# Hybrid mLSTM/HGRN2 step on one core: later transposes and mixing in the mains, more early output blocks, and v's gate weights behind the projected block

## The chip, the cores and the metric

The kernel runs on one core of one Trainium2 chip. Such a core has five engines that each work through their own instructions in order: TensorE (PE: matmuls and transposes, with its weight loads as PEld), VectorE (DVE), ScalarE (ACT), GpSimd (POOL) and SyncE (SP), which here only issues DMAs. Tiles lie in SBUF (128 partitions), matmuls write to PSUM banks, and inputs, outputs and scratch tensors lie in HBM. The metric is the device time of one launch in microseconds (us); lower is better.

## What is computed

One decoder layer on a prompt of 1024 tokens and on 8 samples of 8 tokens, 1088 rows of width 1024 in all. After an RMSNorm, one projection gives seven groups of 1024 columns; four mLSTM heads and eight HGRN2 heads run as causal recurrences, evaluated in chunks; both are normalised, gated, joined and projected back.

```python
xn = rmsnorm(x, g_norm)
xm, zm, om, fh, qh, ih, zh = split(xn @ w_in)
xc = silu(causal_conv(xm, conv_buf, conv_w, conv_b))
q, k, v = per_head(xc @ w_q), per_head(xc @ w_k), per_head(xm @ w_v)
gates = concat(q, k, v) @ w_gate + b_gate
hm, C1, n1, m1 = mlstm_scan(q, k, v, gates[:4], log_sigmoid(gates[4:]), C0, n0, m0)
hm = (layernorm(hm) * sigmoid(om) + m_skip * xc) * silu(zm)
logf = log(lb + (1 - lb) * sigmoid(fh))
oh, S1 = hgrn2_scan(silu(qh), (1 - lb) * sigmoid(-fh), ih, logf, S0)
oh = rmsnorm(oh) * silu(zh)
y = rmsnorm(x + concat(hm, oh) @ w_out, g_final)
```

The outputs are y for prompt and samples, and the new convolution rows, C, n, m and S of both.

## The kernel before

**Arithmetic.** float32 products are made of splits: each operand is a rounded high part plus a rest, and `mm3` (L94 to L96) sums three matmuls, high x high, rest x high, high x rest. ScalarE rounds (the high part); GpSimd or VectorE subtracts (the rest).

**Front.** The normalised rows lie transposed and split in XH and XL. A block is 128 columns of `w_in`: `in_block` runs 24 matmuls in each of three stretches of tokens (384, 384, 320) and hands the bank to an evacuation. For each mLSTM head the two xm blocks are projected and convolved (`front_conv`); v is made from xm (`front_v`), q and k from the convolved xc (`front_qk`), and all three go to HBM. `qkv_prep(h)` loads and splits the head's weights, and folds the gate weights into eight further columns of v's weights: four transposes of w_v (L394), a copy (wT, L395), two matmuls (L398), a copy (gv, L401), two transposes back (L403), and two VectorE passes into the split weights (L405, L406). `front_v` (L488) then finds the gates' part of v in columns 256 to 264 of its bank; VectorE copies or adds it into GTOK (L505, L507) while ScalarE copies v (L503).

**Mains.** Twelve mains follow, in the order H0 M0 H1 M1 H2 M2 H3 M3 H4 H5 H6 H7. `mlstm_main` runs eight chunk steps with the state C (split into CC, L749 and L750), a `layer_norm` of each step's result into a tile hn (L657), its transposes (`turn_back`, L719) and the product onto om (L724); then the samples' stage (transposes L811, state updates L821 to L825), and at its end, for two feature tiles, the mixing: load xcr, multiply-add with om (VectorE, L837), multiply with zm (GpSimd, L839), store to mixd. `hgrn_main` starts with Q and K (L972, L973, L937), a first run of small matmuls (L101, called by `burst`), then `products(n)` for n = 2 to 64 (VectorE: L1005, L940, L1008, L1010), the matmuls of the lower levels (2, 4, 8), of the upper levels (16, 32, 64), and then state, outputs and norms. `gate_scan` runs its scans on VectorE beside the first main.

**Order.** In the mains TensorE's order is written by hand: `weave` takes a main, which yields after each piece the matmul time that should follow it, and emits that much (times a ratio) of the side work, which is the next job's projection blocks, 48 pieces a main. The ratio is the side's cost over the main's sum of yields (`HEAD`, 47.2 for H and 53.4 for M, plus an extra where other work is woven in), so that both end together. The other engines' order comes from a scheduler that simulates the program ahead of time and goes by the order in which instructions were emitted, as far as buffers and operands allow; it is fixed in the program, and `issue_after` adds an edge to it on one engine. Outside the mains TensorE's order comes from it too.

**Buffers.** Large tiles come from one pool of 18 units; PSUM has three pools, mm (3 banks, projections and output accumulators), lv (2) and o (3). Weight and mix loads share three buffers (wraw).

**Output.** The output projection sums 15 mixed tiles from HBM and the last head's z from SBUF, in two column halves (hf) and nine row blocks (t). Five blocks of the first half are begun beside the last main (`early_out`): their accumulators are closed and stored as partial sums for t = 0 and 1 (`out_store`), and stay open in the three mm banks for t = 2 to 4. After the last main, `out_done(0, t)` adds the last tile, the residual and the sum of squares (L1318, L1322), and the blocks t = 5 to 8 follow one by one from t = 2 on, each with a load of the second half's weights (`wo_prep`). `wo_split` (L1241) subtracts on GpSimd for odd tiles of the first half, else on VectorE.

Of the kernel before, what the change touches and what calls it, by code (L numbers as in the profile page):

```python
# [9 lines left out]
F32 = mybir.dt.float32  # L10
# [20 lines left out]
def hybrid_step(  # L31
# [345 lines left out]
    def qkv_prep(h):  # L377

        wr = qkv_load(h)
        wh = unit("wqh", F32R)  # L380
        wl = unit("wql", F32R)
        whv, wlv = vcols(wh), vcols(wl)
        wrv = wr[:, 512:1024].rearrange("p (a c) -> p a c", c=256)
        S.copy(wh[:, :512], wr[:, :512])
        S.copy(whv[:, :, :256], wrv)
        G.tensor_tensor(wl[:, :512], wr[:, :512], f32(wh[:, :512]), op=ALU.subtract)
        G.tensor_tensor(wlv[:, :, :256], wrv, f32(whv[:, :, :256]), op=ALU.subtract)
        qkv_w[h] = (wh, wl)
        wT = half("wT")
        pt = ps_o()  # L390
        for b in range(2):
            for a in range(2):
                o, i = 512 + a * 256 + b * P, b * 2 + a
                PE.transpose(pt[:, i * P:(i + 1) * P], wr[:, o:o + P], ident)  # L394
        V.tensor_copy(wT[:, :512], pt)  # L395
        pg = ps_o()
        for b in range(2):
            PE.matmul(pg[:8, :256], lhsT=wgr[:, 8 + 2 * h + b, :], rhs=wT[:, b * 256:(b + 1) * 256],  # L398
                      start=b == 0, stop=b == 1)
        gv = sp.tile([P, 256], F32, tag="hn", name=nm("gv"), bufs=3)  # L400
        V.tensor_copy(gv[:8, :], pg[:8, :256])  # L401
        for a in range(2):
            PE.transpose(pg[:, 256 + a * 8:264 + a * 8], gv[:8, a * P:(a + 1) * P], ident[:8, :8])  # L403
        pgv = pg[:, 256:272].rearrange("p (a c) -> p a c", c=8)
        V.tensor_copy(whv[:, :, 256:264], pgv)  # L405
        V.tensor_tensor(wlv[:, :, 256:264], pgv, f32(whv[:, :, 256:264]), op=ALU.subtract)  # L406

    GTOK = cp.tile([P, 9, 8], F32, name="GTOK")

# [78 lines left out]
    def front_v(h):  # L488
        wh, wl = qkv_w[h]
        xms = [fr[2 * h + a]["m"] for a in range(2)]  # L490
        for t in range(9):
# [12 lines left out]
            if h:  # L504
                V.tensor_tensor(GTOK[:, t, :], GTOK[:, t, :], ps[:, 256:264], op=ALU.add)  # L505
            else:
                V.tensor_copy(GTOK[:, t, :], ps[:, 256:264])  # L507
            if t == 8:
                nc.sync.dma_start(out=vsd[h], in_=vt[:, :VW])
            elif u:  # L510
                nc.sync.dma_start(out=vd[h, :, (t - 1) * VW:(t + 1) * VW], in_=vt[:, :2 * VW])

# [28 lines left out]
    def gate_scan():  # L541
# [21 lines left out]
        yield 4.0  # L563
# [14 lines left out]
        yield 4.0  # L578
# [80 lines left out]

    def mlstm_main(h):  # L660
# [70 lines left out]
        C = tp = hn = None  # L731
        for j in range(8):
# [18 lines left out]
            if j > 0:  # L751
                if j % 2:
                    tp = ps_lv()
                turn_back(hn, tp, (j - 1) % 2)
                if j % 2 == 0:
                    onto_om(tp, j // 2 - 1)
            hn = layer_norm(pn, j, h)
# [3 lines left out]
            yield 2.8 if j else 4.2  # L761
        turn_back(hn, tp, 1)
        onto_om(tp, 3)
# [32 lines left out]
        yield 5.0  # L796
        pn = ps_o()
# [10 lines left out]
        yield 3.0  # L808
        tp = ps_lv()
        for a in range(2):  # L810
            PE.transpose(tp[:, a * P:(a + 1) * P], hn[:, a * P:(a + 1) * P], ident)  # L811
        for a in range(2):
            oms, ts = compact(d["om"][a][:, TP:T]), spread(tp[:, a * P:(a + 1) * P])
            for e in range(2):
                V.scalar_tensor_tensor(oms[:, e], ts[:, e], mln[:, 2 * h + a:2 * h + a + 1], oms[:, e],
                                       op0=ALU.mult, op1=ALU.mult)
        for a in range(4):
# [9 lines left out]
            yield 1.3  # L827
# [4 lines left out]
        for a in range(2):  # L832
# [3 lines left out]
            with tc.issue_after(getattr(new, "ins", new)):  # L836
                V.scalar_tensor_tensor(xc[:, :T], xc[:, :T], msk[:, ft:ft + 1], d["om"][a][:, :T],  # L837
                                       op0=ALU.mult, op1=ALU.add)
            G.tensor_tensor(xc[:, :T], xc[:, :T], d["zm"][a][:, :T], op=ALU.mult)  # L839
            nc.sync.dma_start(out=mixd[ft], in_=xc[:, :T])  # L840
            yield 1.8
# [75 lines left out]
    def hgrn_main(h):  # L917
# [78 lines left out]
        small_out(ps, 288, 1, 1)  # L996
        yield 1.0
# [61 lines left out]
        for n in (2, 4, 8):  # L1059
            lower.append(products(n))  # L1060
            yield 3.3
# [172 lines left out]
    def wo_split(hf, i):  # L1234
# [6 lines left out]
        (G if hf == 0 and i % 2 else V).tensor_tensor(lo, raw, f32(hi), op=ALU.subtract)  # L1241
# [38 lines left out]
    def out_part(hf, t, g):  # L1280
# [6 lines left out]
        for k in range(len(mx)):  # L1287
            stop = (hf, t, g, k) in ((0, 0, 1, 6), (0, 1, 1, 6))
# [10 lines left out]
    def out_store(t):  # L1299

        if t == 0:
            part[1] = unit("xr")
        part[t] = part[1][:, t * HU:(t + 1) * HU]
# [48 lines left out]
    HEAD = {"H": 47.2, "M": 53.4}  # L1352
# [20 lines left out]
    EARLY = 5  # L1373

    def early_out():
        for t in range(EARLY):
# [5 lines left out]
            if t < EARLY - 3:  # L1382
                out_store(t)

    side = chain(*[(hgrn_in if kind == "H" else mlstm_in)(h) for kind, h in jobs], early_out())
    qkv_prep(0)
    run(front_conv(0, (0, 1)))
    for h in range(4):
        front_v(h)
        if h < 3:  # L1390
            qkv_prep(h + 1)
        if h < 3:
            run(front_conv(h + 1, (2 * h + 2,)))
        else:
# [9 lines left out]
    with tc.manual_schedule(engines={mybir.EngineType.PE}):  # L1404
        for i, (kind, h) in enumerate(jobs[:-1]):
            main = (hgrn_main if kind == "H" else mlstm_main)(h)
            extra = 0.0
            if i == 0:
                main, extra = with_gates(main, gates), 9.0
            weave(islice(side, STEPS), main, us / (HEAD[kind] + extra))  # L1410
        weave(side, hgrn_main(7), (us / 2 + EARLY * cost(45, 512)) / HEAD["H"])
        for t in range(9):
            out_done(0, t)
            if EARLY - 3 <= t < 6:
                run(chain(out_part(0, t + 3, 0), out_part(0, t + 3, 1)))
# [97 lines left out]
```

## Time and profile before

| | |
|---|---|
| median of 3 runs | 1219.85 us (1218.01 to 1223.15) |
| the profiled execution's own time | 1220.89 us |
| its span in the trace | 1219.1 us |
| instructions | 22869 |
| mean granted TensorE clock | 0.983 |
| bytes read from and written to HBM | 93.96 and 38.43 MB |

The span runs from the first to the last instruction in the trace. A row of TensorE's waits names the waiting tile and line, then the engine, tile and line that released it, and gives the total, the number and the longest wait. Windows give busy time by engine in a stretch and the clock that TensorE was granted in it (1.00 is full speed). A row of the timeline gives start and length in us, engine, line, the tiles, and in brackets the idle time just before it with what ended it; rows with "xN" are several instructions merged.

### The profile page before, as it was taken

The numbers are of one execution on the slowest core, as the hardware profiler recorded it, in microseconds if no ns is written. First come the engines' busy times: TensorE is split into PE (matmuls) and PEld (weight loads), VectorE is DVE, ScalarE is ACT, GpSimd is POOL, SyncE is SP. The second block draws the span as 40 slices with busy tenths as digits, with TensorE's granted clock in tenths as the row PEclk, the third lists the DMA queues.
The fourth block names the chain that finished last, engine by engine and source line by source line (L and its number), as shares of the span: only waits on it lengthen the run. The fifth ranks groups of instructions, "written<-read, shape, count | busy, mean of one in ns | idle before, by whom it ended". The sixth has DMA issues, their size and how long they took to land. (4 is left out here: it accounts for less than half of the span.)

```text
span 1219.1 us, 22869 instructions
## 1 busy us (share of the span) xinstructions
PE 1139.4 (93%) x9251; PEld 1064.6 (87%) x9251; DVE 771.5 (63%) x1474; ACT 437.4 (36%) x937; POOL 389.3 (32%) x508
## 2 busy tenths in 40 slices
PE   6899999979988999899998999899999989989997
PEld 5789999979988998899988998899999978767886
DVE  4674544595669466875669466876868686533443
ACT  5454444425321443134321453142424233333332
POOL 4443333223434343523434352533232331100000
PEclk9899999999999999999999999999999999989999
DMA  8133334123133232414132331412121245556652
GB/s 262 45 129 134 129 122 135 35 54 125 60 115 107 84 114 74 148 53 146 34 120 98 110 106 57 143 54 73 53 74 53 73 143 141 166 157 180 210 175 99
DMA packets 154061, 133.89 MB, mean 110 GB/s; under 512 B 11439, under 2 KB 130155, under 8 KB 153954
## 3 DMA queue, kind: packets, MB, share of 16 engines
q1 hardware_dynamic: 153954, 132.41, 34.6%
q8 instruction: 73, 1.20, 0.4%
q14 instruction: 34, 0.28, 0.1%
HBM read 93.96 MB, written 38.43 MB: 109 GB/s over the span
## 5 line engine op out<-in xcount | busy, mean ns | idle before, releaser
L94 PE MATMUL mm<-XH,whi 128*128 128x384 f32 (+1 forms) x1344 | 454.3, 338 | 0.9 <-DVE z L880 0.6
L95 PE MATMUL mm<-XL,whi 128*128 128x384 f32 (+1 forms) x1344 | 442.6, 329 | 0.0
L96 PE MATMUL mm<-XH,wlo 128*128 128x384 f32 (+1 forms) x1344 | 442.1, 329 | 0.0
L94 PEld LDWEIGHTS mm<-XH,whi 128*128 128x128 f32 x1344 | 255.7, 190 | 5.7 <-issue 1.7
L95 PEld LDWEIGHTS mm<-XL,whi 128*128 128x128 f32 x1344 | 255.9, 190 | 1.7 <-issue 1.3
L96 PEld LDWEIGHTS mm<-XH,wlo 128*128 128x128 f32 x1344 | 255.0, 190 | 0.0
L147 POOL TENSOR_TENSOR wlo<-wraw,whi 128x1024 fp32r<-128x1024 f32 x56 | 139.5, 2491 | 226.5 <-ACT whi L147 226.0
L147 ACT CAST whi<-wraw 128x1024 fp32r<-128x1024 f32 x56 | 58.9, 1051 | 123.4 <-PE mm L95 104.5
L94 PE MATMUL mm<-XH,mhi 128*128 128x512 f32 x144 | 59.2, 411 | 10.1 <-ACT lv L1322 4.6
L96 PE MATMUL mm<-XH,mlo 128*128 128x512 f32 x144 | 57.8, 401 | 1.2 <-DVE mlo L1267 1.2
L1266 ACT CAST mhi<-mraw 128x1024 fp32r<-128x1024 f32 (+1 forms) x32 | 31.9, 998 | 74.7 <-PE mm L95 56.2
L95 PE MATMUL mm<-XL,mhi 128*128 128x512 f32 x144 | 57.7, 401 | 0.0
L1335 POOL TENSOR_TENSOR rs<-rs,mhalf 128x1 f32<-128x1 f32 (+1 forms) x9 | 4.9, 542 | 158.3 <-DVE rs L1334 158.3
L1267 DVE TENSOR_TENSOR mlo<-mraw,mhi 128x1024 fp32r<-128x1024 f32 (+1 forms) x32 | 39.0, 1221 | 24.0 <-ACT mhi L1266 23.8
L940 DVE TENSOR_TENSOR QK<-hk,Sf 128x256 f32<-128x256 f32 x96 | 49.4, 555 | 0.0
L457 DVE TENSOR_TENSOR xml<-mm,xmh 128x384 fp32r<-128x384 f32 (+1 forms) x24 | 12.1, 508 | 52.2 <-ACT XB L456 45.0
L872 DVE TENSOR_SCALAR f<-f,OML,LB 128x384 f32<-128x384 f32 (+1 forms) x24 | 26.8, 1116 | 27.2 <-ACT f L870 27.1
L94 PEld LDWEIGHTS mm<-XH,mhi 128*128 128x128 f32 x144 | 27.9, 194 | 17.2 <-issue 5.0
L1008 DVE TENSOR_TENSOR Sf<-Sf,f 128x512 f32<-128x512 f32 (+1 forms) x48 | 40.1, 836 | 0.1
L892 ACT COPY iT<-mm 128x128 f32<-128x128 f32 x64 | 13.0, 270 | 73.3 <-PE mm L96 70.3
L473 DVE SCALAR_TENSOR_TENSOR Y<-XB,PAR,Y 128x1112 f32<-128x1112 f32 x24 | 38.1, 1589 | 0.2
L96 PE MATMUL mm<-woh,mlo 128*128 128x512 f32 x96 | 37.5, 391 | 0.3 <-DVE mlo L1267 0.3
(350 smaller groups left out, 2237.0 us busy)
## 6 DMA issues: line engine op xcount, KB each, us to landing
wraw<-in_w_in SPq DMA_DIRECT2D x56, 512.0 KB, 4.2
woraw<-in_w_out SPq DMA_DIRECT2D x16, 512.0 KB, 4.4
mraw<-mixd SPq DMA_DIRECT2D x16, 512.0 KB, 6.2
mraw<-mixd SPq DMA_DIRECT2D x16, 448.0 KB, 4.5
xcd<-XB SPq DMA_DIRECT2D x8, 544.0 KB, 2.7
qkd<-qk SPq DMA_DIRECT2D x16, 272.0 KB, 5.0
xcr<-xcd SPq DMA_DIRECT2D x8, 544.0 KB
mixd<-xcr SPq DMA_DIRECT2D x8, 544.0 KB
```

Source lines behind the costliest of these rows:

```text
L94: PE.matmul(out, lhsT=lh, rhs=rh, start=first, stop=False)
L95: PE.matmul(out, lhsT=lh, rhs=rl, start=False, stop=False)
L96: PE.matmul(out, lhsT=ll, rhs=rh, start=False, stop=last)
L147: return S.copy(hi, raw), G.tensor_tensor(lo, raw, f32(hi), op=ALU.subtract)
L457: V.tensor_tensor(ml[:, t0:t0 + m], ps[:, :m], f32(mh[:, t0:t0 + m]), op=ALU.subtract)
L473: V.scalar_tensor_tensor(Y[:, :1112], XB[:, j:j + 1112], cw[:, 8 * j + ft:8 * j + ft + 1], Y[:, :1112], op0=ALU.mult, op1=ALU.add)
L872: V.tensor_scalar(f[:, s], f[:, s], scalar1=OML[:, h:h + 1], scalar2=LB[:, h:h + 1], op0=ALU.mult, op1=ALU.add)
L892: S.copy(dst, ps[:, u * P:(u + 1) * P])
L940: i = V.tensor_tensor(dst, ksrc, ssrc, op=ALU.mult)
L1008: V.tensor_tensor(hv(Sf, W, n)[:, :, 0, :], hv(Sf, W, n)[:, :, 0, :], hv(f, W, n)[:, :, 1, n - 1:n].to_broadcast([P, ng, n]), op=ALU.mult)
L1266: S.copy(hi[:, :w * n], raw[:, :w * n])
L1267: V.tensor_tensor(lo[:, :w * n], raw[:, :w * n], f32(hi[:, :w * n]), op=ALU.subtract)
```

## The change

It touches six places.

- `qkv_prep` becomes a generator of two parts: loads and splits first, v's gate columns second. The caller emits the second part behind the block that is projected meanwhile (for head 0 behind both xm blocks).
- `front_v`: ScalarE copies the gate columns, into GTOK for head 0, else into a new tile GST, which VectorE adds to GTOK once at the end.
- `mlstm_main`: each hn is transposed two steps later instead of one, the last one behind the samples' preparation; the samples' transposes go between their state updates; the yields change, and the mixing leaves the main as two deferred pieces.
- `hgrn_main` takes up these pieces behind products(2) and products(4) when it follows an mLSTM main, with 1.8 of yield each (an extra of 3.6).
- `gate_scan` yields 5.5 twice instead of 4.0 (the first main's extra: 12 instead of 9).
- Output: VectorE subtracts in every `wo_split`; four early blocks are stored instead of two, two in a unit; the later blocks begin behind `out_done(0, 3)`.

```diff
     def qkv_prep(h):
...
         qkv_w[h] = (wh, wl)
+        yield
         wT = half("wT")
...
         V.tensor_tensor(wlv[:, :, 256:264], pgv, f32(whv[:, :, 256:264]), op=ALU.subtract)
+        yield
     def front_v(h):
...
             S.copy(vv[:, u, 0:256], ps[:, :256])
-            if h:
-                V.tensor_tensor(GTOK[:, t, :], GTOK[:, t, :], ps[:, 256:264], op=ALU.add)
-            else:
-                V.tensor_copy(GTOK[:, t, :], ps[:, 256:264])
+            S.copy((GST if h else GTOK)[:, t, :], ps[:, 256:264])
...
+        if h:
+            V.tensor_tensor(GTOK, GTOK, GST, op=ALU.add)
     def gate_scan():
-        yield 4.0
+        yield 5.5
...
-        yield 4.0
+        yield 5.5
     def mlstm_main(h):
-        C = tp = hn = None
+        C = tp = None
+        hns = []
         for j in range(8):
...
-            if j > 0:
+            if j > 1:
+                if j % 2 == 0:
+                    tp = ps_lv()
+                turn_back(hns.pop(0), tp, j % 2)
                 if j % 2:
-                    tp = ps_lv()
-                turn_back(hn, tp, (j - 1) % 2)
-                if j % 2 == 0:
                     onto_om(tp, j // 2 - 1)
-            hn = layer_norm(pn, j, h)
+            hns.append(layer_norm(pn, j, h))
...
-            yield 2.8 if j else 4.2
-        turn_back(hn, tp, 1)
-        onto_om(tp, 3)
+            yield 2.8
+        tp = ps_lv()
+        turn_back(hns.pop(0), tp, 0)
...
         yield 5.0
+        turn_back(hns.pop(0), tp, 1)
+        onto_om(tp, 3)
...
         hn = layer_norm(pn, 8, h)
-        yield 3.0
-        tp = ps_lv()
-        for a in range(2):
-            PE.transpose(tp[:, a * P:(a + 1) * P], hn[:, a * P:(a + 1) * P], ident)
...
+        yield 2.0
         for a in range(4):
...
-            yield 1.3
+            if a == 1:
+                tp = ps_lv()
+                for b in range(2):
+                    PE.transpose(tp[:, b * P:(b + 1) * P], hn[:, b * P:(b + 1) * P], ident)
+                for b in range(2):
+                    oms, ts = compact(d["om"][b][:, TP:T]), spread(tp[:, b * P:(b + 1) * P])
+                    for e in range(2):
+                        V.scalar_tensor_tensor(oms[:, e], ts[:, e], mln[:, 2 * h + b:2 * h + b + 1], oms[:, e],
+                                               op0=ALU.mult, op1=ALU.mult)
+            yield 1.5
...
-        for a in range(2):
+        def mixed(a):
             ft = 2 * h + a
             xc = unit("xcr")
             nc.sync.dma_start(out=xc[:, :T], in_=xcd[ft])
-            with tc.issue_after(getattr(new, "ins", new)):
-                V.scalar_tensor_tensor(xc[:, :T], xc[:, :T], msk[:, ft:ft + 1], d["om"][a][:, :T],
-                                       op0=ALU.mult, op1=ALU.add)
+            V.scalar_tensor_tensor(xc[:, :T], xc[:, :T], msk[:, ft:ft + 1], d["om"][a][:, :T],
+                                   op0=ALU.mult, op1=ALU.add)
             G.tensor_tensor(xc[:, :T], xc[:, :T], d["zm"][a][:, :T], op=ALU.mult)
             nc.sync.dma_start(out=mixd[ft], in_=xc[:, :T])
-            yield 1.8
+        deferred.extend([lambda: mixed(0), lambda: mixed(1)])
     def hgrn_main(h):
+        late = [deferred.pop(0) for _ in range(len(deferred))]
         yield 1.0
...
         for n in (2, 4, 8):
             lower.append(products(n))
+            if late:
+                with tc.issue_after(getattr(lower[-1][3], "ins", lower[-1][3])):
+                    late.pop(0)()
+                yield 1.8
             yield 3.3
     def wo_split(hf, i):
-        (G if hf == 0 and i % 2 else V).tensor_tensor(lo, raw, f32(hi), op=ALU.subtract)
+        V.tensor_tensor(lo, raw, f32(hi), op=ALU.subtract)
     def out_part(hf, t, g):
-            stop = (hf, t, g, k) in ((0, 0, 1, 6), (0, 1, 1, 6))
+            stop = hf == 0 and t < STORED and (g, k) == (1, 6)
     def out_store(t):
-        if t == 0:
-            part[1] = unit("xr")
-        part[t] = part[1][:, t * HU:(t + 1) * HU]
+        if t % 2 == 0:
+            ctxs["xr"] = unit("xr")
+        part[t] = ctxs["xr"][:, t % 2 * HU:(t % 2 + 1) * HU]
-    HEAD = {"H": 47.2, "M": 53.4}
+    HEAD = {"H": 47.2, "M": 48.2}
-    EARLY = 5
+    EARLY, STORED = 5, 4
     def early_out():
-            if t < EARLY - 3:
+            if t < STORED:
                 out_store(t)
-    qkv_prep(0)
+    prep = qkv_prep(0)
+    next(prep)
     run(front_conv(0, (0, 1)))
+    run(prep)
     for h in range(4):
         front_v(h)
         if h < 3:
-            qkv_prep(h + 1)
+            prep = qkv_prep(h + 1)
+            next(prep)
             run(front_conv(h + 1, (2 * h + 2,)))
+            run(prep)
...
             extra = 0.0
+            if kind == "H" and i and jobs[i - 1][0] == "M":
+                extra = 3.6
             if i == 0:
-                main, extra = with_gates(main, gates), 9.0
+                main, extra = with_gates(main, gates), 12.0
             weave(islice(side, STEPS), main, us / (HEAD[kind] + extra))
...
             out_done(0, t)
-            if EARLY - 3 <= t < 6:
-                run(chain(out_part(0, t + 3, 0), out_part(0, t + 3, 1)))
+            if 3 <= t < 7:
+                run(chain(out_part(0, t + 2, 0), out_part(0, t + 2, 1)))
```

More of the change, by code (lines that the diff above doesn't have):

```diff
@@ L406, in qkv_prep @@
         V.tensor_tensor(wlv[:, :, 256:264], pgv, f32(whv[:, :, 256:264]), op=ALU.subtract)
+        yield
     GTOK = cp.tile([P, 9, 8], F32, name="GTOK")
+    GST = cp.tile([P, 9, 8], F32, name="GST")
     def gate_part(h, qk, ready):
@@ L658, in layer_norm @@
         return hn
+    deferred = []
     def mlstm_main(h):
@@ L807, in mlstm_main @@
         hn = layer_norm(pn, 8, h)
-        yield 3.0
-        tp = ps_lv()
-        for a in range(2):
-            PE.transpose(tp[:, a * P:(a + 1) * P], hn[:, a * P:(a + 1) * P], ident)
-        for a in range(2):
[L813 to L816, printed above, removed]
+        yield 2.0
         for a in range(4):
@@ L831, in mlstm_main @@
             G.tensor_copy(NEWv[:, h, 4 * i:4 * i + 4], C0v[i][:, :, 256])
-        for a in range(2):
+        def mixed(a):
             ft = 2 * h + a
@@ L1390, in hybrid_step @@
         if h < 3:
-            qkv_prep(h + 1)
-        if h < 3:
+            prep = qkv_prep(h + 1)
+            next(prep)
             run(front_conv(h + 1, (2 * h + 2,)))
+            run(prep)
         else:
```

## The prediction

> **What bounds the kernel now.** I read the first part of the page, then TensorE's own view of waits, then windows around each wait for the granted clock.
>
> ```profile
> span 1219.1 us, 22869 instructions
> PE 1139.4 (93%) x9251; PEld 1064.6 (87%) x9251; DVE 771.5 (63%) x1474; ACT 437.4 (36%) x937; POOL 389.3 (32%) x508
> ```
>
> TensorE is busy for 1139.4 of 1219.1 us. The change takes no matmul away, so all it can win lies in the 79.7 us in which TensorE stands, and in slow clock around these gaps. TensorE's waits (us in total, times, longest):
>
> ```profile
> PE lv L719 <- DVE hn L657: 15.3, 16, 1.6
> PE lv L101 <- DVE K L937: 13.3, 4, 3.3
> ...
> PE mm L94 <- ACT lv L1322: 4.6, 1, 4.6
> PE lv L101 <- DVE QK L1005: 4.6, 2, 2.8
> PE mm L94 <- DVE z L880: 4.3, 3, 3.7
> PE o L398 <- DVE wT L395: 2.9, 2, 2.1
> PE mm L94 <- DVE GTOK L507: 2.7, 2, 2.2
> PE lv L811 <- DVE hn L657: 2.7, 4, 0.7
> ...
> PE mm L94 <- DVE xr L1318: 1.7, 2, 0.9
> ...
> PE mm L94 <- DVE GTOK L505: 1.3, 4, 0.6
> PE mm L1276 <- DVE xr L1318: 1.1, 1, 1.1
> ```
>
> Each of these lines belongs to one part of the change. The windows (length, busy time of PE, PEld, DVE, ACT, POOL, then PEclk, DMA share, GB/s) show what follows a gap:
>
> ```profile
> 36.00:46.00 10.00, 7.54 (x43) 5.44 (x42) 6.62 (x20) 5.14 (x13) 3.37 (x17) 0.70 0.18 52
> 60.00:68.00 8.00, 5.85 (x33) 5.08 (x32) 5.24 (x10) 3.94 (x9) 3.83 (x3) 0.79 0.40 132
> 264.00:274.00 10.00, 5.95 (x116) 5.21 (x114) 8.43 (x14) 3.02 (x10) 3.68 (x8) 0.83 0.40 107
> 786.00:792.00 6.00, 5.95 (x98) 5.82 (x99) 5.93 (x14) 0.00 (x0) 1.28 (x3) 0.72 0.31 90
> 990.00:1000.00 10.00, 6.32 (x24) 5.04 (x23) 9.90 (x19) 2.10 (x2) 0.08 (x1) 0.83 0.39 121
> 1066.00:1074.00 8.00, 4.65 (x11) 3.71 (x12) 3.20 (x6) 2.41 (x8) 0.00 (x0) 0.59 0.86 269
> ```
>
> A clock of 0.72 over 6 us is 0.28 x 6 = 1.7 us of work not done; in the same way 3.0, 1.7, 1.7, 1.7 and 3.3 us in the others, of which some falls on idle time.
>
> **The mLSTM mains (four of them).** Before, the transposes of step j's normalised tile (L719) are emitted in step j+1; now in j+2, and the sample's (L811) two matmul pairs later. What a step gets between is its yield times the weave's ratio: 2.8 x 47.4/53.4 = 2.5 us before, 2.8 x 47.4/48.2 = 2.75 us now (47.4 us is what the kernel's own cost formula gives for four blocks, 4 x 24 matmuls over 1088 columns). The longest wait on hn is 1.6 us, so one whole step more covers it: 15.3 + 2.7 = 18.0 us go. What is late next is the split state CC, which step j+1 multiplies:
>
> ```profile
> 719.26 0.73 DVE L750 TENSOR_TENSOR CC<-C,CC 128x258 fp32r<-128x258 f32 x1
> ...
> 721.44 0.28 PE L94 MATMUL o<-CC,qgl 128*128 128x258 f32 x1
> ```
>
> It is there 1.45 us ahead in step 1, where the step shrinks from 4.2 x 47.4/53.4 = 3.7 us to 2.75: 1.0 us less, just enough. These waits also gave VectorE time to catch up, so I let 1 us per main come back: bounds 0 and 3 us; 14 us net.
>
> **From an mLSTM main to the next HGRN2 main.** L101 waits 3.3 us four times. VectorE's order there, and then the same entry where no mLSTM main stands before it:
>
> ```profile
> 774.51 1.35 DVE L837 SCALAR_TENSOR_TENSOR xcr<-xcr,PAR,om 128x1088 f32<-128x1088 f32 x1
> ...
> 776.24 3.40 DVE L837 SCALAR_TENSOR_TENSOR xcr<-xcr,PAR,om 128x1088 f32<-128x1088 f32 x1
> ...
> 777.13 0.31 PE L96 MATMUL mm<-XH,wlo 128*128 128x320 f32 x1
> ...
> 779.56 0.47 DVE L880 TENSOR_TENSOR hq<-hq,mm 128x320 f32<-128x320 f32 x1
> 780.07 2.76 DVE L973 TENSOR_TENSOR Q<-hq,f 128x544 f32<-128x544 f32 x1
> 782.75 3.11 DVE L937 COPY K<-hk 128x256 f32<-128x256 f32 x2
> ...
> 786.01 0.65 PE L101 MATMUL lv<-Q,K 128*32 128x64 f32 x32 [3.34 <-DVE K L937]
> ```
>
> ```profile
> 845.74 2.18 DVE L973 TENSOR_TENSOR Q<-hq,f 128x544 f32<-128x544 f32 x1
> ...
> 847.85 1.19 DVE L937 COPY K<-hk 128x256 f32<-128x256 f32 x2
> ```
>
> The two L837 (1.35 + 3.40) stand ahead of the last hq, of Q and of K. The change takes them out. hq's block ends on TensorE at 777.4, and with half a microsecond for ScalarE's half (an estimate: VectorE's is 0.47) hq could start at 777.95, 1.6 us earlier than it did. K's copies shrink from 3.11 towards 1.19, Q from 2.76 towards 2.18: 2.5 us more, 4.1 in all against a wait of 3.34. TensorE comes 5.0 x (1.004 - 0.933) = 0.35 us sooner, as the entry's yield has a lower ratio (47.4/50.8). I take a rest of 0.3 us: 3.0 us each, and the 1.7 us of slow clock behind it: 4.7 x 4 = 19 us.
>
> The Trainium skill (TensorE: Matmul & The Clock Gate, "Why this matters for your kernels") would have the clock drop only after idle gaps over some 3 us. The trace differs: the window at 264 us holds a longest gap of 2.8 us and a clock of 0.83. By the rule a rest of up to 3 us would still win the clock back; by the trace a rest of 2.8 us would not, and the sum would be 4 x 1.7 = 7 us smaller. A rest of 0.3 wins it by both.
>
> **Where the two L837 go.** They, their two GpSimd multiplies, and on SP's queue their loads and stores now stand in the HGRN2 main, after products(2) and products(4), with 1.8 of yield each. Such a pass costs more than itself, as this pair shows:
>
> ```profile
> 984.88 5.19 POOL L1241 TENSOR_TENSOR XL<-woraw,XH 128x1024 fp32r<-128x1024 f32 x2 [7.50 <-DMA woraw<-in_w_out]
> ...
> 985.18 5.19 DVE L940 TENSOR_TENSOR QK<-hk,Sf 128x256 f32<-128x256 f32 x2
> ...
> 993.38 1.22 DVE L1241 TENSOR_TENSOR XL<-woraw,XH 128x1024 fp32r<-128x1024 f32 x1
> ```
>
> VectorE's work stands until GpSimd's pass is through (5.19 beside 5.19). So a deferred pair costs VectorE between 2 x 1.35 = 2.7 and about 2 x (1.35 + 5.19/2) = 7.9 us. Its cover:
>
> ```profile
> 794.22 0.68 DVE L1005 TENSOR_TENSOR QK<-hq,f 128x512 f32<-128x512 f32 x1
> ...
> 801.95 1.16 PE L101 MATMUL lv<-QK 128*32 128x32 f32 x112
> ```
>
> The lower levels' last operand is ready at 794.9, TensorE asks at 801.95: 7.05 us, less 1.7 (the slow clock that is gone) and 0.9 (12.9 of yield at the lower ratio), plus 3.6 x 0.933 = 3.4: 7.8 us. That is just the dearest case, so 0 to 2 us per main; I take 0.5, 2 us in all. Mains and entries together: 14 + 19 - 2 = **31 us** (15 to 37).
>
> **The front.** The waits on wT (2.9) and GTOK (2.7 + 1.3) and the clock of the first two windows (3.0 + 1.7) make 11.6 us.
>
> ```profile
> 41.62 1.88 PE L398 MATMUL o<-wT,front 128*8 128x256 f32 x4 [2.12 <-DVE wT L395]
> ...
> 62.64 0.22 ACT L459 COPY XB<-mm 128x64 f32<-128x64 f32 x1 [3.43 <-DVE xml L457]
> ```
>
> Behind the projected block, the chain transpose, wT, L398, gv, L403, copies has the next block and front_qk to hide in for h = 1 to 3. For h = 0 nothing is left but front_v, which needs it, and the convolution's passes now stand ahead on VectorE: 0 to 6 us come back there. ScalarE gets 36 copies of 8 columns; the nearest row is 0.22 us for 64 columns, so at most 36 x 0.22 = 8 us on an engine that is busy for 36% of the span, in place of 36 VectorE steps on which TensorE waited. Net between -3 and 10; I take **4 us**.
>
> **The gate scan in the first main.** 3 more units of yield, mostly ahead of L1005's two waits (4.6), against a ratio that falls from 0.84 to 0.80: **1 us** (-1 to 4).
>
> **The last HGRN2 main.** The odd GpSimd passes L1241 become VectorE passes of 1.22. The pair above held VectorE for 5.19; two passes of 1.22 and L940's own work (some 0.7, an estimate from the 0.68 of L1005 over as many columns) replace this, 2.0 us less ahead of the z of L880 on which TensorE stood 3.7 us, and part of the 1.7 us of clock: **3.5 us** (0 to 7).
>
> **The output's start.** Four blocks are stored early, not two, so accumulators are free when t = 5 begins.
>
> ```profile
> 1066.33 0.68 DVE L1318 TENSOR_TENSOR xr<-xr,o 128x512 f32<-128x512 f32 x1
> ...
> 1069.35 0.76 PE L94 MATMUL mm<-XH,mhi 128*128 128x512 f32 x1 [4.64 <-ACT lv L1322]
> ```
>
> The 4.6 us, the 1.7 and the 1.1 on xr, and about 2 us of slow clock after 1069 can go, 9.4 us. The fourth out_done still needs the first's bank in a pool of three, which L1318 frees, and one more weight load goes ahead of t = 5's mix load on SP; the two further residual loads go early, beside the last main. **6 us** (1 to 9).
>
> **Sum.** 31 + 4 + 1 + 3.5 + 6 = 45.5 us off the profiled execution, whose time is 1220.9 (its span and 1.8 us around it): 1175.4. The median of the runs is 1219.85, 1 us under it, so 1174 to 1175; I say 1175.
>
> **The rivals.**
> - *VectorE is late in the HGRN2 mains.* The Trainium skill (SBUF — State Buffer, Terms) has VectorE and GpSimd lock each other out for a whole instruction; the 5.19 beside 5.19 agrees. If all four GpSimd passes of a main (two deferred, two weight splits) fall on the products, 2 us of wait and 1.7 of clock return per main: 15 us, 1190. For: cover and price are equal to 0.1 us. Against: the dear case needs every pass to collide. Chance 0.15.
> - *The mains don't pack.* The hn waits reappear on CC and the entries keep their clock loss: 14 us, the 7 of clock and half of the entries' 13 come back: 27, 1203. Against: all but one step gets longer. Chance 0.08.
> - *The front's chain lies open* for h = 0, with slow clock after it: 7 us back, 1182. Chance 0.07.
> - *Slower: the deferred load is stuck on SP.*
>
> ```profile
> 785.06 14.55 SPq L140 DMA_DIRECT2D wraw<-in_w_in  x2
> ```
>
> SP issues in order and here stands 14.55 us before a weight load can go. If the second xcr load is issued behind it, VectorE stands at L837 with the products queued behind, and TensorE at the lower levels. From 12 us of net wait per main all is lost; with 14.55 less what is left of the cover after the passes (0 to 2), it is 13 x 4 + 7 of clock after longer gaps = 59 us: 1234. Against: the row waits for a weight buffer; a load whose own buffer is free earlier is issued ahead of it. Chance 0.06. A milder form gives back about all: 1216, 0.04.
>
> **How the numbers follow.** The forecast has 0.60; its own range is 1165 to 1186. Faster by over 0.5% (about what a measurement can tell from no change): 0.60 + 0.15 + 0.08 + 0.07 = 0.90; within: 0.04; slower: 0.06. The range 1162 to 1203 leaves out the last two rivals and the best corner, some 0.15.
>
> **What would show it.** Right: hn L657 and K L937 gone from TensorE's waits, the entry windows at clock 1.00, L837 between the products, no wait of L101 at the lower levels, no GTOK or wT, no L1322 near the output's start. Wrong: new rows of L101 behind QK or xcr, of L94 behind CC, a gap before front_v(0), or xcr as VectorE's releaser by a DMA.

## The result, and the profile after

| | before | after |
|---|---|---|
| median | 1220.7 us (1218.0 to 1223.2, 4 runs) | 1190.6 us (1188.6 to 1191.6, 4 runs) |
| after / before | | 0.975, 95% interval 0.973 to 0.978 |
| span of the profiled execution | 1219.1 us | 1188.1 us |

The kernel became 30 us faster. The forecast was 1175 us with a range of 1162 to 1203, so the time lies in the range, and 15.6 us above the forecast: almost on the 1190 us of the first rival.

The head of the page after:

```profile
span 1188.1 us, 22927 instructions
PE 1130.5 (95%) x9251; PEld 1062.1 (89%) x9251; DVE 782.3 (66%) x1447; ACT 441.1 (37%) x973; POOL 381.9 (32%) x504
```

VectorE is busy for 10.8 us longer than before (771.5), with 27 instructions fewer. That is the first hint. TensorE's waits after (released by; us in total, times, longest):

```profile
...
PE lv L1123 <- ACT A L1066: 10.5, 5, 3.2
PE lv L101 <- DVE QK L950: 7.9, 4, 2.2
PE mm L94 <- DVE z L890: 6.2, 1, 6.2
...
PE mm L95 <- DVE wql L407: 2.2, 1, 2.2
PE o L399 <- DVE wT L396: 2.1, 1, 2.1
PE mm L94 <- DVE wqh L406: 1.4, 1, 1.4
PE lv L101 <- DVE K L947: 1.1, 1, 1.1
```

Most rows that the change aimed at are gone: no hn (18.0 us before), K only once, no GTOK, no wait at the output's start (L1322 and xr before). The wait for head 0's wT is still there, 2.1 us as before. In place of the others stand two rows that come five and four times, in the HGRN2 mains: the upper levels' end (L1123) behind A, and the lower levels (L101) behind QK. wqh and wql are new in the front, and there is one wait of 6.2 us for z, in the first main, where there were three with 4.3 in all.

Where the gain arose can be read from marks in TensorE's timeline: the first small matmul of a HGRN2 main (`lv<-Q,K`), the first matmul of an mLSTM main (`lv<-q,k`), and the first of `out_done` (`o<-XH,zh`). All numbers are us of the profiled executions.

| stage, from mark to mark | before | after | change | predicted |
|---|---|---|---|---|
| front, to H0 | 231.08 | 230.15 | -0.9 | -4 |
| H0 with the gate scan, to M0 (302.81; 303.17) | 71.73 | 73.02 | +1.3 | -1 |
| M0 to H5 (849.18; 833.13) | 546.37 | 529.96 | -16.4 | -31 |
| H5 to H7 (974.80; 958.78) | 125.62 | 125.65 | 0.0 | 0 |
| H7 to `out_done` (1062.51; 1040.90) | 87.71 | 82.12 | -5.6 | -3.5 |
| `out_done` to the end | 156.59 | 147.20 | -9.4 | -6 |
| sum | 1219.1 | 1188.1 | -31.0 | -45.5 |

The whole gap lies in one row: M0 to H5, 14.6 us short. The front and the first main missed by 5.4 us, the last two stages made that good by 5.5. Within M0 to H5 an mLSTM main with its side work went from 75.6 us (M1: 514.13 - 438.58) to 65.4 (499.60 - 434.17), while the HGRN2 main ahead of it went from 60.5 (438.58 - 378.11) to 65.4 (434.17 - 368.73). Between its marks the HGRN2 main runs six of the projection's matmuls more (282 for 276), which is about 1 us; the other 4 us are loss.

The timeline of after in H3, a main that took up the two mixing pieces (start, length, engine, line, tiles; in brackets the idle time ahead and its releaser):

```profile
628.67 2.17 DVE L983 TENSOR_TENSOR Q<-hq,f 128x544 f32<-128x544 f32 x1
630.76 1.20 DVE L947 COPY K<-hk 128x256 f32<-128x256 f32 x2
...
635.52 1.35 DVE L846 SCALAR_TENSOR_TENSOR xcr<-xcr,PAR,om 128x1088 f32<-128x1088 f32 x1 [0.66 <-DMA xcr<-xcd]
...
636.95 2.54 POOL L848 TENSOR_TENSOR xcr<-xcr,zm 128x1088 f32<-128x1088 f32 x1 [3.83 <-DVE xcr L846]
...
637.16 2.92 DVE L1019 TENSOR_TENSOR Sf<-Sf,f 128x544 f32<-128x544 f32 x1
...
642.39 0.71 DVE L1019 TENSOR_TENSOR Sf<-Sf,f 128x544 f32<-128x544 f32 x1
...
643.78 1.34 DVE L846 SCALAR_TENSOR_TENSOR xcr<-xcr,PAR,om 128x1088 f32<-128x1088 f32 x1
...
645.20 2.92 POOL L848 TENSOR_TENSOR xcr<-xcr,zm 128x1088 f32<-128x1088 f32 x1 [5.71 <-DVE xcr L846]
...
645.64 5.26 DVE L950 TENSOR_TENSOR QK<-hk,Sf 128x256 f32<-128x256 f32 x2
...
648.09 2.53 POOL L147 TENSOR_TENSOR wlo<-wraw,whi 128x1024 fp32r<-128x1024 f32 x1
...
650.96 0.46 PE L101 MATMUL lv<-QK 128*32 128x32 f32 x32 [1.79 <-DVE QK L950]
...
652.61 0.75 DVE L950 TENSOR_TENSOR QK<-hk,Sf 128x256 f32<-128x256 f32 x2
```

The entry is as forecast: Q 2.17 and K 1.20, no wait. Then come the pieces. Beside the first multiply L848, L1019 takes 2.92 us where its twin takes 0.71. Beside the second one and the weight split right behind it (2.92 + 2.53), the two L950 take 5.26 where they take 0.75 seven us later. What TensorE waits for at 650.96 is exactly this L950. So in this main VectorE lost 1.35 + 1.34 to the pieces themselves, 0.66 to the load, 2.2 and 4.5 to being held: 10.1 us, of which some 2.5 belong to the weight split. The prediction had 7.9 as the dearest price against 7.8 of cover.

The second half of the same main:

```profile
660.86 2.40 POOL L147 TENSOR_TENSOR wlo<-wraw,whi 128x1024 fp32r<-128x1024 f32 x1
...
661.03 2.77 DVE L1021 TENSOR_TENSOR f<-f 128x512 f32<-128x512 f32 x1
...
666.45 0.28 DVE L1103 TENSOR_TENSOR Vs<-V,Vs 128x128 fp32r<-128x128 f32 x1
...
666.77 1.28 ACT L1107 ACTIVATE VL<-Vs,CF 128x128 fp32r<-128x128 f32 x4 [4.11 <-DVE Vs L1103]
667.96 1.80 ACT L1066 COPY A<-lv 32x128 f32<-32x128 f32 x6
...
669.81 0.66 PE L1123 MATMUL lv<-CF,iT 128*128 128x128 f32 x4 [2.70 <-ACT A L1066]
```

VectorE is still late, and a second weight split holds it again (L1021 takes 2.77 us where it took 0.69 nine us earlier), so Vs comes late; ScalarE stands 4.11 us for it with VL at the head of its queue, and the copies of A (L1066) are queued behind VL. TensorE's row names ScalarE, but ScalarE was itself held by VectorE.

Windows of after (length; PE, PEld, DVE, ACT, POOL busy; clock; DMA share; GB/s):

```profile
763.00:769.00 6.00, 6.00 (x111) 5.97 (x112) 5.41 (x9) 0.60 (x3) 1.42 (x3) 1.00 0.71 256
...
669.00:677.00 8.00, 7.19 (x52) 7.19 (x53) 3.31 (x10) 4.08 (x9) 1.14 (x2) 1.00 0.03 6
802.00:810.00 8.00, 8.00 (x41) 8.00 (x42) 3.01 (x9) 2.38 (x7) 0.00 (x0) 0.63 0.00 0
...
303.20:833.10 529.90, 511.74 (x4484) 498.31 (x4482) 393.08 (x811) 180.23 (x417) 219.37 (x267) 0.99 0.30 97
```

The entry of H4 has the full clock (0.72 before), but the clock now falls behind the new wait in the same main, 0.63 over 8 us, 3.0 us of work not done; in H3, at 669 us, it held. The last row is the stretch M0 to H5, and here it is for the kernel before:

```profile
302.80:849.20 546.40, 515.06 (x4493) 499.61 (x4493) 378.59 (x811) 178.68 (x416) 215.18 (x267) 0.99 0.29 95
```

TensorE stands for 546.4 - 515.1 = 31.3 us before and 18.2 after. VectorE executes 811 instructions in both, but is busy 14.5 us longer.

### The profile page after: what moved, and what is told of

Same layout as the page of the kernel before. It is cut to its first block, busy times and chain, and to the rows that moved or that the text cites. A ratio compares the mean times of both kernels' runs of the same rounds, so it can differ in the third digit from the quotient of the medians.

```text
span 1188.1 us, 22927 instructions
## 1 busy us (share of the span) xinstructions
PE 1130.5 (95%) x9251; PEld 1062.1 (89%) x9251; DVE 782.3 (66%) x1447; ACT 441.1 (37%) x973; POOL 381.9 (32%) x504
## 4 chain that ended last, share of the span: by engine, by line
PE 54%; DVE 13%; DMA 5%; ACT 2%; issue 2%; POOL 0%; SPq 0%; POOLq 0%; DVEq 0%; ACTq 0%
PE mm L94 14%; PE mm L96 14%; PE mm L95 14%; DVE QK L950 3%; DVE Sf L1019 2%; DVE f L1021 2%; DMA xcr<-xcd 2%; DMA woraw<-in_w_out 2%; PE o L1169 1%; DMA mraw<-mixd 1%; DVE QK L1016 1%; PE o L1188 1%; PE o L95 1%; PE o L94 1%; PE o L96 1%
## 5 line engine op out<-in xcount | busy, mean ns | idle before, releaser
L94 PE MATMUL mm<-XH,whi 128*128 128x384 f32 (+1 forms) x1344 | 454.0, 338 | 6.5 <-DVE z L890 6.2
L94 PEld LDWEIGHTS mm<-XH,whi 128*128 128x128 f32 x1344 | 255.6, 190 | 10.3 <-DVE z L890 6.3
L94 PE MATMUL mm<-XH,mhi 128*128 128x512 f32 x144 | 57.2, 397 | 0.5 <-ACT mhi L1281 0.5
L950 DVE TENSOR_TENSOR QK<-hk,Sf 128x256 f32<-128x256 f32 x96 | 56.2, 625 | 0.0
L1019 DVE TENSOR_TENSOR Sf<-Sf,f 128x512 f32<-128x512 f32 (+1 forms) x48 | 46.5, 969 | 0.1
L882 DVE TENSOR_SCALAR f<-f,OML,LB 128x384 f32<-128x384 f32 (+1 forms) x24 | 32.1, 1338 | 19.5 <-ACT f L880 19.3
L1021 DVE TENSOR_TENSOR f<-f 128x512 f32<-128x512 f32 (+1 forms) x48 | 42.2, 879 | 0.8
L1060 POOL COPY A<-A 32x32 f32<-32x32 f32 x16 | 14.3, 891 | 85.2 <-DVE A L977 84.8
L94 PE MATMUL mm<-woh,mhi 128*128 128x512 f32 x96 | 37.4, 389 | 0.0
```

The costliest lines, as they stand in the source:

```text
L94: PE.matmul(out, lhsT=lh, rhs=rh, start=first, stop=False)
L882: V.tensor_scalar(f[:, s], f[:, s], scalar1=OML[:, h:h + 1], scalar2=LB[:, h:h + 1], op0=ALU.mult, op1=ALU.add)
L950: i = V.tensor_tensor(dst, ksrc, ssrc, op=ALU.mult)
L1019: V.tensor_tensor(hv(Sf, W, n)[:, :, 0, :], hv(Sf, W, n)[:, :, 0, :], hv(f, W, n)[:, :, 1, n - 1:n].to_broadcast([P, ng, n]), op=ALU.mult)
L1021: V.tensor_tensor(hv(f, W, n)[:, :, 1, :], hv(f, W, n)[:, :, 1, :], hv(f, W, n)[:, :, 0, n - 1:n].to_broadcast([P, ng, n]), op=ALU.mult)
L1060: G.tensor_copy(A[64 * g:64 * g + 32, TP + 32 * g:TP + 32 * g + 32], A32[64 * g:64 * g + 32, 256:288])
```

## The experiments

The theory: the deferral of the mixing into the products, priced at 2 us in the forecast, cost some 15 us. The rivals: the mains did not pack, or the load of xcr held VectorE (its wait above is 0.66 us, and 1.8 us in the four mains together, which speaks against it at once), or the missing time is in the front and the gate scan. The ratios are to the kernel before, with 95% intervals; edits are against the changed kernel unless said otherwise.

**The pieces later (mix_late).** Same deferral, same yields, other places: behind the last VectorE pass into KS and behind the last state.

```diff
         for n in (2, 4, 8):
             lower.append(products(n))
-            if late:
-                with tc.issue_after(getattr(lower[-1][3], "ins", lower[-1][3])):
-                    late.pop(0)()
-                yield 1.8
             yield 3.3
...
-                    V.tensor_tensor(KS[r, c], pt[r, :P], f32(KS[r, c]), op=ALU.subtract)
+                    ks = V.tensor_tensor(KS[r, c], pt[r, :P], f32(KS[r, c]), op=ALU.subtract)
+        if late:
+            with tc.issue_after(getattr(ks, "ins", ks)):
+                late.pop(0)()
+            yield 1.8
...
+        if late:
+            with tc.issue_after(getattr(sn, "ins", sn)):
+                late.pop(0)()
+            yield 1.8
```

> The two deferred mixing passes stand behind the upper levels: one after the splits of KS, one after the states, each with its 1.8 of yield; all else as in the changed kernel. Theory: VectorE works without a break from the entry of an HGRN2 main to the upper levels (628 to 667 us in the changed kernel's trace), so the two L846 and the GpSimd multiplies that hold it up are what makes L101 wait on QK L950 (7.9 us in four) and L1123 wait on A L1066 (10.5 us in five). Then both rows all but vanish, three losses of clock go, and the time falls by 14 to 20 us, to 1171 to 1177. Rival: VectorE has too much to do over mains and HGRN2 mains together, and the waits move to the outputs or to the next mLSTM main: 1186 to 1194. Second rival: the buffers of om and zm, held longer, keep the next blocks waiting: over 1195.

Measured: 1172.9 us, 0.960 (0.958 to 0.963), as the theory had it. Of its waits, and its stretch M0 to H5:

```profile
PE mm L94 <- DVE z L890: 6.3, 1, 6.3
PE lv L1119 <- ACT A L1066: 4.5, 5, 2.2
```

```profile
303.60:817.30 513.70, 506.59 (x4489) 493.80 (x4490) 379.51 (x811) 180.86 (x417) 215.17 (x267) 1.00 0.31 100
```

No row of L101 behind QK is left, and that of A fell from 10.5 to 4.5 us. TensorE stands 7.1 us in the stretch (18.2 in after), and is busy 5.2 us less, which with the same matmuls points to the clock. VectorE is busy 13.6 us less for the same 811 instructions: it was held, not working. From mark to mark the stretch takes 817.26 - 303.63 = 513.6 us, 32.7 less than before. The place of the pieces decides it in every profile: the stretch takes 527.3 to 530.0 us in the seven kernels here that have them behind the products with the multiply on GpSimd, and 507.6 to 513.6 in the three that have them late (mix_late, and late_old and late_pin below).

**The mixing back in the mLSTM main (mix_back).** The pieces run at the mLSTM main's end as before, again held behind its last state update; the re-spacing stays.

```diff
...
-        deferred.extend([lambda: mixed(0), lambda: mixed(1)])
+        for a in range(2):
+            mixed(a)
+            yield 1.8
...
-    HEAD = {"H": 47.2, "M": 48.2}
+    HEAD = {"H": 47.2, "M": 51.8}
...
-                extra = 3.6
+                extra = 0.0
```

> The mixing alone goes back to the end of the mLSTM main (1.8 of yield each there, none in the HGRN2 main); the later transposes and all else stay as in the changed kernel. Theory: the deferral won the entry's wait (3.3 us and 1.7 us of clock, four times: 20 us) and gave 4.5 us and some clock of it back per main (about 18 to 22 us in all): taking it back changes little, 1186 to 1198, with K L947 back among TensorE's waits at about 13 us and QK and A gone. Rival, the prediction's working: the deferral is worth 17 us net, so 1207 or more.

Measured: 1177.1 us, 0.965 (0.962 to 0.967). Both expectations missed: it is 13 us faster than the changed kernel. The deferral as it was made is a loss against leaving the mixing where it was. Its row of waits at the entries (H0's 1.1 us is in it), and windows at H1, H2, H3 and H4 and over the stretch:

```profile
PE lv L101 <- DVE K L950: 9.4, 5, 2.1
```

```profile
372.00:378.00 6.00, 5.79 (x108) 5.68 (x109) 5.90 (x15) 0.60 (x3) 1.43 (x3) 1.00 0.32 90
500.00:506.00 6.00, 5.91 (x99) 5.79 (x100) 5.90 (x14) 0.00 (x0) 1.34 (x3) 0.72 0.32 90
629.00:635.00 6.00, 5.57 (x96) 5.45 (x97) 5.90 (x15) 0.00 (x0) 1.68 (x4) 0.72 0.33 90
758.00:764.00 6.00, 5.14 (x94) 5.03 (x95) 5.90 (x12) 0.00 (x0) 2.10 (x4) 0.72 0.31 90
...
303.40:821.90 518.50, 510.03 (x4490) 498.54 (x4488) 368.24 (x811) 179.04 (x416) 222.18 (x266) 0.99 0.31 100
```

The entry waits returned, but at 2.07 us each, not 3.3: the forecast had priced the entries as if only the deferral could shorten them. From M0 to H5 it takes 821.94 - 303.35 = 518.6 us, so in these profiles the late place of the pieces (mix_late) is worth 5.0 us over no deferral, not the 19 that the forecast gave the entries. The intervals of the two medians just overlap, so the amount is uncertain; the profiles of late_old and late_pin have 9 to 11.

**The multiply on VectorE (mix_dve).** This takes GpSimd's two passes out of the products and leaves VectorE's own work there, 1.29 us more of it a piece.

```diff
-            G.tensor_tensor(xc[:, :T], xc[:, :T], d["zm"][a][:, :T], op=ALU.mult)
+            V.tensor_tensor(xc[:, :T], xc[:, :T], d["zm"][a][:, :T], op=ALU.mult)
```

> The deferred multiply runs on VectorE instead of GpSimd, in the same place; all else as in the changed kernel. Theory: GpSimd's two passes of 2.5 us hold VectorE's work up beside them (L1019 takes 2.92 instead of 0.71 us, the pair of L950 5.26 instead of 0.75 us with a weight split behind); on VectorE a pass costs 1.2 us. So VectorE gains about 2 us per main, and the waits on QK L950 shrink from 2 us to 0 to 1: 3 to 8 us faster, 1182 to 1187. Rival: the wait is VectorE's work itself, or the xcr load in front of L846, and not GpSimd: no change, 1189 to 1192.

Measured: 1182.0 us, 0.968 (0.966 to 0.970), the fast end of what the theory had. Of its waits:

```profile
PE lv L1123 <- ACT A L1066: 12.2, 5, 3.2
```

The row of QK is gone, that of A stayed. So about half of the 17.7 us that mix_late won is GpSimd's multiplies, which collide ahead of the lower levels. The other half stays with VectorE's own passes at a place where it has no room; that is by elimination, and no run takes those away alone. The two weight splits on GpSimd hold VectorE in both: in H3 L1021 takes 2.80 and 2.77 us in mix_dve, and in mix_late L1019 takes 2.89 and L1093 2.31.

**The gate scan's yields (gate4)**: 4.0 twice again, with the extra of 9.

```diff
-        yield 5.5
+        yield 4.0
```

> The gate scan's two yields go back from 5.5 to 4.0 and the first main's extra from 12 to 9; all else as in the changed kernel. Theory: the 6.2 us wait on z L890 in the first main comes from the three banks of projections, all held by blocks of z that VectorE reaches only behind the scan; more matmuls ahead of it only fill the banks sooner, so the wait and its clock (6.8 us at half) go back to the two waits of before: 2 to 4 us faster, 1186 to 1189. Rival, the prediction's working: the longer yields cover the scan, and without them it is 1 to 2 us slower, 1192.

Measured: 1191.3 us, 0.976 (0.974 to 0.978): no difference from the changed kernel, so the theory's 2 to 4 us were wrong, and the rival's 1 to 2 us slower are not shown either. The wait only moved:

```profile
PE lv L101 <- DVE QK L1016: 1.8, 1, 1.8
...
PE mm L94 <- DVE z L890: 1.3, 2, 0.8
```

A wait of 3.25 us for A in the same main comes with them, where it was 0.75. The stage H0 took 75.6 us in this profile, against 73.0 in the changed kernel's and 71.7 before; among all profiles here it is 71.7 to 75.6 with the yields of 4.0 and 72.9 to 75.5 with those of 5.5, so the +1.3 of the table can't be told from this spread.

**The front (front_old, gate_dve, resp_only, front_only).** The front has two edits, so there are four kernels on the new mains, and one that has the front's edits alone on the kernel before.

```diff
-    prep = qkv_prep(0)
-    next(prep)
+    run(qkv_prep(0))
     run(front_conv(0, (0, 1)))
-    run(prep)
```

is front_old (for the later heads likewise);

```diff
-            S.copy((GST if h else GTOK)[:, t, :], ps[:, 256:264])
+            if h:
+                V.tensor_tensor(GTOK[:, t, :], GTOK[:, t, :], ps[:, 256:264], op=ALU.add)
+            else:
+                V.tensor_copy(GTOK[:, t, :], ps[:, 256:264])
```

is gate_dve; resp_only has both, and front_only has neither, on the kernel before.

> As the changed kernel (1190.6 us), but each head's weights for q, k, v and the gates are prepared in one piece ahead of the convolution again; ScalarE still copies v's gate columns. Theory (the moved piece's last steps stand behind the convolution's passes on VectorE, and TensorE waits 1.4 us for wqh and 2.2 us for wql in place of the waits for wT and GTOK of before): these two go, a wait for wT of about 2 us a head stays where the order puts it; 0 to 3.6 us faster, 1187 to 1190.6. Rival (moving the piece is worth its 1.8 us a head, as the prediction's front term has it): 2 to 5 us slower, 1192.5 to 1195.5.

> As the changed kernel, but VectorE copies and adds v's gate columns out of the bank again (no GST); the piece-wise preparation stays. Theory (the short ScalarE copies free the accumulators, and the waits for GTOK of 4.0 us in all with one stretch of half clock are what they save): 2 to 6 us slower, 1193 to 1196.5. Rival (TensorE is held at that place by VectorE's conversions of the next weights anyway): within 1 us, 1189.5 to 1191.5.

> As the changed kernel (1190.6 us) without both parts of its front: the weights of a head are prepared in one piece ahead of the convolution, and VectorE copies and adds v's gate columns; the re-spaced mains and the output alone are left. Theory (the piece behind the block costs 4 us, as the run with the piece undone showed, and ScalarE's copies save little, as the run with VectorE's showed): 1185.5 to 1189. Rival (without the piece-wise preparation the waits for GTOK of before, 4.0 us and a stretch of half clock, return and ScalarE's copies are what saves them): 1190 to 1194.

> The kernel before (1220.3 us) with the two parts of the front alone: weights prepared in two pieces around the convolution, ScalarE copies v's gate columns, GST added by one VectorE instruction a head. The prediction's front term: 4 us faster, 1216 (from 10 us faster to 3 us slower). Theory now (the waits for wT and GTOK are replaced by waits for wqh and wql behind the convolution's passes): within 2 us, 1218 to 1222.

| on the new mains | ScalarE copies | VectorE copies |
|---|---|---|
| weights in two pieces | 1190.6, 0.975 (0.973 to 0.978) | 1190.8, 0.976 (0.975 to 0.978) |
| weights in one piece | 1186.3, 0.972 (0.971 to 0.974) | 1193.7, 0.978 (0.975 to 0.981) |

front_only: 1222.5 us, 1.001 (0.999 to 1.003), no difference from the kernel before. By the theories: front_old came out just past the fast end of its theory, gate_dve and resp_only missed theirs and met their rivals, and front_only met its theory, no gain. One piece with ScalarE's copies is just apart from both kernels with VectorE's copies, not from the changed kernel (0.971 to 0.974 against 0.973 to 0.978). The same windows in the four, in the order front_old, resp_only, the changed kernel, gate_dve:

```profile
50.00:70.00 20.00, 17.62 (x119) 15.80 (x118) 11.93 (x16) 10.12 (x30) 8.64 (x6) 0.99 0.28 86
```

```profile
50.00:70.00 20.00, 16.76 (x109) 15.32 (x108) 12.63 (x22) 10.28 (x23) 9.27 (x7) 0.91 0.32 103
```

```profile
50.00:70.00 20.00, 16.39 (x99) 14.79 (x98) 12.31 (x17) 9.68 (x26) 9.15 (x7) 0.83 0.28 90
```

```profile
50.00:70.00 20.00, 15.88 (x93) 14.05 (x93) 12.38 (x21) 9.40 (x20) 9.17 (x7) 0.83 0.28 91
```

The clock is whole only with one piece and ScalarE's copies. With two pieces wqh and wql stand behind the convolution's passes on VectorE, and beside their waits (1.4 and 2.2 us, at 58 and 62 us) the clock loses 0.17 x 20 = 3.4 us. Yet in its profile front_old reaches H0 at 230.95, 0.8 us later than after, because other half-clock stretches fell elsewhere (0.93 from 70 to 90 us). The 4 us between the medians are therefore not shown to lie in the front: of the 3.6 us between the two profiles, M0 to H5 has 2.3, H7 1.0 and the output 1.8, where the edit changes nothing, and up to M0 front_old is 1.5 later.

**The last main and the output (wo_pool, stored2).**

```diff
-        V.tensor_tensor(lo, raw, f32(hi), op=ALU.subtract)
+        (G if hf == 0 and i % 2 else V).tensor_tensor(lo, raw, f32(hi), op=ALU.subtract)
```

```diff
-    EARLY, STORED = 5, 4
+    EARLY, STORED = 5, 2
...
-            if 3 <= t < 7:
-                run(chain(out_part(0, t + 2, 0), out_part(0, t + 2, 1)))
+            if 2 <= t < 6:
+                run(chain(out_part(0, t + 3, 0), out_part(0, t + 3, 1)))
```

> As the changed kernel, but GpSimd makes the low part of every second tile of the output weights' first half again. Theory (its passes of about 2 us hold VectorE's in the last HGRN2 main, where TensorE waits for what VectorE makes; the prediction priced it 0 to 7 us, and the stage gained 5.6 us): 2 to 6 us slower, 1192.5 to 1196.5. Rival (VectorE has room in the last main, and the 5.6 us come from the accumulators that are put aside): within 1 us, 1189.5 to 1191.5.

> As the changed kernel, but only two of the five early accumulators are put aside, and the next token tiles' first products start a step earlier, from t = 2, with three steps' distance, as before. Theory (the output's gain of 9 us is the accumulators' waits L1322 and the waits for the transfers of xr, with their clock): 5 to 10 us slower, 1196 to 1201. Rival (the gain there comes from the last main's shorter tail and the split on VectorE): within 2 us, 1188.5 to 1192.5.

wo_pool: 1192.9 us, 0.978 (0.976 to 0.979), not told apart from the changed kernel by its time; its stage H7 to `out_done` took 1045.66 - 959.63 = 86.0 us against 82.1, which is the theory's place and size. This stage hardly varies otherwise: 81.1 to 82.5 us in the eleven kernels where VectorE subtracts, 86.0 to 87.7 in the three where GpSimd does. stored2: 1198.5 us, 0.982 (0.979 to 0.985), slower as the theory had it. Its last stage took 1191.9 - 1037.6 = 154.3 us against 147.2 (145.4 to 147.2 in the eleven kernels that store four blocks, 154.3 to 156.6 in the three that store two), and the waits are back:

```profile
PE mm L94 <- ACT lv L1337: 3.5, 1, 3.5
...
PE mm L94 <- DVE xr L1333: 1.7, 2, 0.9
...
PE mm L1291 <- DVE xr L1333: 1.1, 1, 1.1
```

**Together (late_old, late_pin).** late_old is mix_late with the weights in one piece; late_pin besides puts the gate scan's second part behind the first main's KS.

```diff
-            if i in (1, 4, 11, 13):
+            if i in (1, 11, 12, 13):
...
+        ctxs["pin"] = getattr(ks, "ins", ks)
...
+        with tc.issue_after(ctxs["pin"]):
             V.tensor_tensor(st, st, m[:, 0:TP].rearrange("p (b c) -> p b c", c=P)[:, 0:7, 127], op=ALU.add)
             V.tensor_copy(lfs, lm[0:4, :])
             V.tensor_tensor_scan(b, t1, lf, initial=0.0, op0=ALU.mult, op1=ALU.add)
             V.tensor_tensor(y, b, m, op=ALU.subtract)
```

> Two changes together: the deferred mixing behind the products' last readers (behind KS and behind the states of the HGRN2 main), which alone gave 1172.9 us, and the weights' preparation in one piece, which alone gave 4.3 us. Theory (they concern different stages and add up): 1167 to 1170.5. Rival (the piece's gain came from where half-clock stretches fell in the stages that the other edit has cleared): 1171 to 1174.

> As the kernel with the late mixing and the one-piece preparation; besides the gate scan's second part (the running sum over 4 rows and three passes over 4 rows, 6 us of VectorE) is emitted and held behind the first HGRN2 main's KS, where VectorE is busy 1.4 of each 5 us. Theory (TensorE's wait of 6.3 us for z in the first HGRN2 main is VectorE's queue of level passes and gate scan, and half clock follows it): 5 to 9 us faster than the kernel that it is made from, 1159 to 1165. Rival (VectorE's level passes fill that stretch by themselves, and the wait only takes another place): within 1.5 us of it, 1167 to 1172.

late_old: 1169.2 us, 0.958 (0.955 to 0.961). The number is the theory's, but its interval overlaps that of mix_late, so that the two edits add up is not shown. late_pin: 1168.2 us, 0.957 (0.954 to 0.961): the rival held. The wait for z (6.3 us in mix_late's profile, 2.0 in late_old's) is gone, and two others stand in the same main (of the first row, 3.1 us):

```profile
PE lv L1120 <- ACT A L1067: 4.3, 2, 3.1
...
PE lv L101 <- DVE QK L1017: 3.3, 2, 2.1
```

Both beat the changed kernel by 21 to 22 us.

## Why the prediction was right, and where it was off

The sign and the range held; the amount was 30 of 45.5 us. By its steps:

- **The mLSTM mains.** Right, and better than forecast. The waits on hn are gone, no row of L94 behind CC came, so the 1 us a main that was to come back did not. With the pieces out of the products' way (mix_late), M0 to H5 gains 32.7 us; the forecast had 14 + 19 = 33 ahead of the deferral's price. That this sum fits so well is partly luck, as its parts do not: the re-spacing alone gains 27.8 us (mix_back), where the forecast had 14, and the deferral at the late place adds 5 to 11, where it had 19.
- **The entries.** Q, K, the wait and the clock came out as worked out (2.17 and 1.20 in H3, no wait, 1.00). But the term was credited to the deferral whole, and mix_back shows that the re-spacing alone brings the wait from 3.3 to 2.07 us.
- **"Where the two L837 go" is the step that failed.** It priced the deferral at 2 us; it cost 32.7 - 16.4 = 16.3. Its cover was about right: 10.1 us of price less the wait of 1.8 leaves 8.3, against 7.8. Its price was not. It took half of a GpSimd pair's 5.19 us for each piece as the dearest case, where each pass held VectorE's next one to its end, and a weight split hung on behind. And it looked at one due point only, the lower levels' operand. VectorE stays late up to the upper levels, where the wait of 9.8 us for A of H1 to H4 (10.5 with H0's 0.75) is the larger one; mix_dve, which takes the multiplies' collisions away and keeps VectorE's passes, still has it (12.2).
- **The first rival** named this: all passes on the products, 15 us, 1190. Its time came within 1 us, and its mechanism is that of the lower levels. The upper levels were not in it, and took the place of part of the clock loss that was. Cover and price equal to 0.1 us was a reason to give it more than 0.15.
- **The front.** Forecast 4, came 0.9 in the stage, which varies by more than that, and nothing alone (front_only 1.001). Of the 11.6 us that it counted as the prize, the waits were 6.9; 5.7 us of waits stand there after, the wT of head 0 among them (2.1). The prediction saw that the convolution's passes would stand ahead of h = 0's chain and gave 0 to 6 us for it; the waits are wqh and wql, 3.6 us. It expected ScalarE's copies to help on their own; they do with one piece, where the intervals are apart, not with two.
- **The gate scan.** Forecast 1 us faster (from 1 slower to 4 faster), 1.3 slower in the profile, which is within the stage's spread, and no difference by gate4. VectorE is busy without a break at that place (late_pin: 4.95 to 5.00 of each 5 us from 236 to 266 us), so spacing moves the wait and does not remove it.
- **The last main and the output.** Forecast 3.5 and 6, came 5.6, within its range of 0 to 7, and 9.4, just above its range of 1 to 9 (the prediction had counted 9.4 us that can go and discounted them); wo_pool and stored2 give back 3.9 and 7.1 of it in the same stages.

Left open: what makes front_old 4 us faster than the changed kernel, how the half of the deferral's cost that GpSimd's multiplies do not make divides up, and whether another place in H0 for the gate scan would win.

## What to carry to other kernels

Before deferring work from a gap where it costs a visible wait into a stretch that looks covered, sum what the receiving engine does up to every later due point, not only the next one, and price each GpSimd pass with two SBUF inputs as a full stop of VectorE's next such pass. Where cover and price come out equal, look for a stretch where the receiving engine is mostly idle: the same two passes cost 16 us more behind the products than a few steps later.

## What the runs showed of the hardware

**GpSimd holds VectorE to the end of its pass, and passes in a row add up**: 5.26 us for two L950 beside 2.92 + 2.53 us of GpSimd, 0.75 without. The Trainium skill (SBUF — State Buffer, Terms) has the shared ports locked for a full instruction; the trace agrees.

**The clock falls after gaps of about 2 us, but not each time.** In mix_back the same wait of 2.07 us at the same place was followed by a clock of 1.00 in H1, and by 0.72 in H2, H3 and H4; in after, 2.70 us at 669.81 left it whole. The Trainium skill (TensorE: Matmul & The Clock Gate, "Why this matters for your kernels") advises against gaps over some 3 us; here shorter ones lost it too. Its Part 1 lets the activity window run freely, some 3.4 us long; by that figure an estimate of one window at half clock is 1.7 us of work. That the same gap had both outcomes, and that the loss here is 0.28 x 6 = 1.7 us, agrees with it.

**One profile of the front is uncertain by 4 us**: front_old and late_old give TensorE the same order up to H0, and their profiles reach it at 230.95 and 227.02, with a clock of 0.83 and 0.91 from 30 to 50 us and of 0.93 and 1.00 from 70 to 90.
